# The duration that a list schedule assumes for a float32r product, raised to the step between products in the trace

## The chip, the cores and the metric

The kernel runs on one core of one Trainium2 chip. The metric is the device time of one execution in microseconds (us), the median of several runs. Lower is better. The core's engines are called by the profile's short names: PE (TensorE, matrix products; PEld is its weight load), DVE (VectorE), ACT (ScalarE), POOL (GpSimd) and SP (SyncE, which here only issues DMAs).

## The reference, cut to what matters

Two transformer blocks follow each other on 256 tokens of width 1024, each block two layers deep, all in float32. A layer of the first block is a feed-forward part, a mixer of four kinds of attention, and a second feed-forward part; a layer of the second block is a mixer of three kinds of attention and one feed-forward part.

```python
def first_block(x, ...):
    for l in range(2):
        x = x + 0.5 * swiglu(rms_norm(x, ffn1_norm[l]), gate1[l], up1[l], down1[l])
        h = rms_norm(x, mix_norm[l]) @ w_in[l]          # 12 pieces: q, k, v of four attentions
        o = concatenate([neighborhood, differential, grouped_query, dilated])
        x = x + o @ w_out[l]
        x = x + 0.5 * swiglu(rms_norm(x, ffn2_norm[l]), gate2[l], up2[l], down2[l])
def second_block(x, c, ...):
    for l in range(2):
        ...  # modulated norm, forget-gate / block-sparse / latent attention, swiglu
def swiglu(h, w_gate, w_up, w_down):
    return (silu(h @ w_gate) * (h @ w_up)) @ w_down
```

## The kernel before, in words

**Products.** Every weight tile is loaded as float32 (`raw`), cut into a high part `whi` (ACT, a cast to float32r) and a low part `wlo` (DVE, `raw - whi`), and the activations are held in two parts as well (`xh`, `xl`). One float32 product is then three float32r products into one PSUM bank (`mm3`): `whi,xh`, `whi,xl`, `wlo,xh`, nearly all 128 x 128 x 512. A weight unit is numbered in the order of use; `WStream` loads three units ahead and splits them in halves of 128 x 1024.

**Stages.** In the feed-forward parts PE runs long rows of products. In a mixer of the first block (two in the program, at about 205 to 345 us and 715 to 860 us of the span; "mixer 0" and "mixer 1" below) the in-projection's products are interleaved with the attention. A chunk of the in-projection goes through `prep`: ACT copies it out (`qk`) and squares it (`qksq`), DVE sums (`ss`, `ms`), POOL multiplies by the gain and takes a power (`rs`), DVE multiplies by `rs`, POOL applies the rotary embedding (`rot`, then `qk` again), PE transposes it (`tp<-ident,qk`), and ACT and DVE split the transpose into high and low part (`qkT`). A head then is a job: PE scores (`att<-qkT`, six products of 256 columns, three per token tile), DVE row maxima (`nm`, or `e` with a bias), ACT exponentials (`pd` or `p`), PE transposes of those, an ACT copy (`pt`), PE products with the values (`att<-V,pt`), and DVE scaling into `o`. The differential heads have two score tiles each and a norm of their own (`ov`, `ovs`, `dss`, and one more POOL power `rs`).

**What sets the order.** The program is first only recorded: `Plan.add` (line 114) stores each operation with its dependencies and a duration in ns from `Plan.cost` (line 145). `Plan.order` (line 182) is a list schedule over that record: for each engine it keeps a clock `now`, and an operation can start at the later of that clock, its inputs' ends plus a hop between engines (`HOP`), and the time its buffer comes free; among the operations that could start within `DELTA` = 60 ns of the earliest, the one of highest priority goes. `Plan.priorities` runs the schedule three times and takes each time the priorities from a backward pass (`backward`) over the same durations. `Plan.issue` (line 300) then issues everything in that order; every recorded instruction has line 304. Each engine works through its own list in order and waits on semaphores. So a duration in `cost` never reaches the chip; it decides only which operation stands before which on each engine.

The lines that the change touches (`self.cold` is a constant tile of the warm-up products, `F32R` is float32r; a product that is neither is plain float32):

```python
if eng == "tensor":
    if method == "transpose":
        return 109, 0, None
    n = kw["rhs"].shape[-1]
    ...
    if kw["rhs"].dtype == F32R:
        return n / 2.4 + 2.5, 0, None
    return 2 * max(107, n / 1.2 + 2), 0, None
```

Of the kernel before, what the change touches and what calls it, by code (L numbers as in the profile page):

```python
# [72 lines left out]
class Plan:  # L73
# [26 lines left out]
    def add(self, eng, method, args, kw):  # L100
# [39 lines left out]
        deps.discard(-1)  # L140
        deps.discard(i)
        cost, after, table = self.cost(eng, method, args, kw, aps)
        self.ops.append([eng, method, args, kw, sorted(deps), sorted(touch), cost, after, table])

    HOP = {"tensor": {"vector": 196, "scalar": 197}, "scalar": {"tensor": 258, "vector": 131, "gpsimd": 169},
           "vector": {"tensor": 254, "scalar": 128, "gpsimd": 155, "vector": 127}, "gpsimd": {"vector": 60, "tensor": 136, "scalar": 100, "gpsimd": 102}}

    def cost(self, eng, method, args, kw, aps):

        if method == "dma_start":  # L150
            return (1000 if eng == "gpsimd" else 475), 4 * int(np.prod(list(args[0].shape))) / 360, None
        n = max(int(np.prod(list(a.shape)[1:])) for k, a in aps)
        psum = any(a.space == PSUM for _, a in aps)
# [4 lines that stand above are left out]
            if kw["rhs"] is self.cold:  # L158
                return 4 * max(107, n / 1.2 + 2), 0, None
            if kw["rhs"].dtype == F32R:  # L160
                return n / 2.4 + 2.5, 0, None
            return 2 * max(107, n / 1.2 + 2), 0, None
        if eng == "scalar":
            extra = 93 * sum(1 for k, _ in aps if k in ("bias", "scale", "accum_out"))
            f = args[2] if len(args) > 2 else kw.get("func")
            return 0.833 * n + (52 if psum else 94) + extra, 0, "silu" if f == AF.Silu else "exp" if f in (AF.Exp, AF.Ln) else None
        if eng == "vector":
            fast = method in ("tensor_copy", "tensor_scalar", "memset") and not psum
            scalars = sum(1 for k, _ in aps if k not in (0, 1, "out", "in_")) if method == "tensor_scalar" else 0
            scalars += sum(1 for k, _ in aps if k == 2) if method == "scalar_tensor_tensor" else 0  # L170
            return n * (0.52 if fast else 1.042) + 68 + 62 * scalars, 0, None
        if eng == "gpsimd":
            if kw.get("op") == ALU.pow:
                return 300 + 165 * n, 0, None
            return 148 + (3.15 if method == "tensor_copy" else 2.11) * n, 0, None
        return 60, 0, None
# [1491 lines left out]
```

## Time and profile before

| | |
|---|---|
| median of 3 runs | 1653.28 us (1652.83 to 1656.73) |
| the profiled execution | 1654.43 us, its span 1652.7 us |
| PE busy | 1627.0 us, 98% of the span |
| DVE, ACT, POOL busy | 1085.4, 842.3, 167.9 us |
| mean granted TensorE clock | 0.989 of 2.4 GHz |
| bytes moved by DMA | 335.78 MB, 203 GB/s |

The span runs from the first to the last instruction of the profiled execution; 1.7 us of its time lie outside. A clock of 1.00 in a stretch is 2.4 GHz, 0.50 is 1.2 GHz, and a number between them is the mean of a stretch that has both. The time that an engine stands idle is put down to whatever released it.

### The profile page before, as it was taken

To read this page: it belongs to the slowest core of one execution; us is meant where nothing else is said; L and a number is where in the kernel's file an instruction comes from. 1 tells how busy PE (TensorE), PEld (TensorE's weight loads), DVE (VectorE), ACT (ScalarE), POOL (GpSimd) and SP (SyncE) were. 2 spreads that over 40 slices of the span, in tenths; PEclk is the share of its full clock that TensorE was granted. 3 is DMA by queue.
4 is the path that set the end of the run, shared out by engine and by line. 5 is a ranking of instruction groups with operands and counts; after the bars stand their busy time and mean duration, and the time that the engine had idled before them with its cause. 6 is when DMAs were issued, how large, how long until landed. Compare 5 with 4: busy or idle time off the path is not lost.

```text
span 1652.7 us, 21333 instructions
## 1 busy us (share of the span) xinstructions
PE 1627.0 (98%) x7912; PEld 1347.2 (82%) x7912; DVE 1085.4 (66%) x1956; ACT 842.3 (51%) x1384; POOL 167.9 (10%) x205
## 2 busy tenths in 40 slices
PE   9989999999999999999999999999999999999998
PEld 7868877888888888877788888888888888888886
DVE  6557778577777877777757645656755476585553
ACT  6544456554434444455554444576644358664442
POOL 0000056000000000035400000120000012000000
PEclk9989999999999999998899999999999999999999
DMA  8687762257776777763328645451645445245451
GB/s 305 221 268 283 264 220 103 77 224 301 267 293 245 300 293 267 289 220 120 110 75 311 245 178 195 171 180 53 242 180 202 153 162 207 101 171 202 176 203 51
DMA packets 81884, 335.78 MB, mean 203 GB/s; under 512 B 17136, under 2 KB 19700, under 8 KB 50676
## 3 DMA queue, kind: packets, MB, share of 16 engines
q1 hardware_dynamic: 81780, 334.42, 55.7%
q8 instruction: 62, 1.02, 0.2%
q14 instruction: 42, 0.34, 0.1%
HBM read 333.29 MB, written 2.84 MB: 203 GB/s over the span
## 4 chain that ended last, share of the span: by engine, by line
PE 92%; DVE 3%; POOL 2%; DMA 1%; issue 1%; ACT 1%; SPq 0%; POOLq 0%; DVEq 0%; ACTq 0%
PE mm L304 54%; PE y L304 27%; PE att L304 6%; PE tp L304 6%; DMA raw<-in_gu 1%; DVE wlo L304 1%; POOL rs L304 1%; POOL qk L304 0%; POOL rot L304 0%; DVE o L304 0%; DVE qk L304 0%; DVE ms L304 0%; DVE xl L304 0%; SPq L304 0%; DMA t5t<-in_t_table 0%
## 5 line engine op out<-in xcount | busy, mean ns | idle before, releaser
L304 DVE TENSOR_TENSOR wlo<-raw,whi 128x1024 fp32r<-128x1024 f32 (+2 forms) x516 | 607.2, 1211 | 263.2 <-ACT whi L304 261.4
L304 ACT CAST whi<-raw 128x1024 fp32r<-128x1024 f32 (+2 forms) x516 | 513.4, 1038 | 316.3 <-PE mm L304 132.1
L304 PE MATMUL mm<-whi,xh 128*128 128x512 f32 (+2 forms) x1376 | 547.0, 398 | 2.5 <-ACT whi L304 1.5
L304 PE MATMUL mm<-wlo,xh 128*128 128x512 f32 (+2 forms) x1376 | 537.3, 391 | 0.7 <-DVE wlo L304 0.7
L304 PE MATMUL mm<-whi,xl 128*128 128x512 f32 (+2 forms) x1376 | 534.8, 390 | 1.6 <-DVE xl L304 1.6
L304 PEld LDWEIGHTS mm<-whi,xl 128*128 128x128 f32 x1376 | 259.9, 189 | 55.7 <-DVE xl L304 2.9
L304 PEld LDWEIGHTS mm<-whi,xh 128*128 128x128 f32 x1376 | 259.9, 189 | 55.3 <-ACT whi L304 2.3
L304 PEld LDWEIGHTS mm<-wlo,xh 128*128 128x128 f32 x1376 | 260.4, 189 | 50.5 <-DVE wlo L304 1.6
L304 PE MATMUL y<-whi,hth 128*128 128x512 f32 x528 | 206.9, 393 | 0.0
L304 PE MATMUL y<-wlo,hth 128*128 128x512 f32 x528 | 206.6, 391 | 0.0
L304 PE MATMUL y<-whi,htl 128*128 128x512 f32 x528 | 206.5, 391 | 0.0
L304 POOL TENSOR_TENSOR rs<-rs,mhalf 128x1 f32<-128x1 f32 x28 | 27.2, 972 | 1267.2 <-DVE rs L304 1267.2
L304 ACT ACTIVATE sil<-mm 128x256 f32<-128x256 f32 x110 | 42.2, 384 | 210.4 <-PE mm L304 209.7
L304 DVE CUSTOM_DVE_ANT_0 ada<-ada,act 128x512 f32<-128x512 f32 x192 | 128.5, 688 | 17.3 <-DMA ada<-in_ada 16.9
L304 PEld LDWEIGHTS y<-wlo,hth 128*128 128x128 f32 x528 | 99.7, 189 | 21.6 <-issue 1.3
L304 PEld LDWEIGHTS y<-whi,htl 128*128 128x128 f32 x528 | 99.7, 189 | 20.9
L304 PEld LDWEIGHTS y<-whi,hth 128*128 128x128 f32 x528 | 99.5, 189 | 20.7 <-ACT whi L304 0.2
L304 DVE TENSOR_TENSOR hch<-mm,sil 128x256 f32<-128x256 f32 x110 | 46.3, 421 | 78.9 <-ACT sil L304 78.5
L304 PE MATMUL att<-qkT 64*128 64x256 f32 (+6 forms) x368 | 65.6, 321 | 1.8 <-DVE qkT L304 1.5
L304 POOL TENSOR_TENSOR rs<-ms,mhalf 128x2 f32<-128x2 f32 (+3 forms) x34 | 50.9, 1499 | 135.8 <-DVE ms L304 134.2
L304 PEld LDWEIGHTS att<-V,pt 128*128 128x128 f32 x448 | 59.5, 196 | 6.3 <-ACT pt L304 2.3
L304 PE MATMUL att<-V,pt 128*128 128x65 f32 (+1 forms) x448 | 60.0, 273 | 1.9 <-ACT pt L304 1.9
(158 smaller groups left out, 1388.1 us busy)
## 6 DMA issues: line engine op xcount, KB each, us to landing
raw<-in_gu SPq DMA_DIRECT2D x127, 1024.0 KB, 4.9
raw<-in_dn SPq DMA_DIRECT2D x66, 1024.0 KB, 4.9
ada<-in_ada SPq DMA_DIRECT2D x192, 256.0 KB, 5.3
raw<-in_in SPq DMA_DIRECT2D x32, 1024.0 KB, 4.8
raw<-in_out SPq DMA_DIRECT2D x16, 1024.0 KB, 4.8
row<-moddram SPq DMA_DIRECT2D x12, 512.0 KB, 6.8
raw<-in_in2a SPq DMA_DIRECT2D x4, 840.0 KB, 4.2
raw<-in_gu SPq DMA_DIRECT2D x6, 512.0 KB, 6.1
```

Of the source, the lines that this page charges most:

```text
L304: getattr(getattr(self.nc, eng), method)(*args, **kw)
```

## The change

One constant in the planner's table is raised. For a product of 512 columns the assumed duration goes from 215.8 to 226.6 ns, for 256 columns from 109.2 to 120.0 ns. No instruction, tile or loop is added or removed; the order on the engines is computed anew.

```diff
             if kw["rhs"].dtype == F32R:
-                return n / 2.4 + 2.5, 0, None
+                return n / 2.4 + 13.3, 0, None
             return 2 * max(107, n / 1.2 + 2), 0, None
```

Three places where the order differs follow. Numbers behind names count tiles and units.

On PE in mixer 0, at the end of the third in-projection chunk (`mm_438`, `mm_459` is the next one), the four transposes of the second differential chunk `qk_424` stand so (- before, + now):

```order
 L304 MATMUL mm_438<-whi38_427,xh_74 128x512
 L304 MATMUL mm_438<-wlo38_428,xh_74 128x512
+L304 MATMUL tp_439<-ident_60,qk_424 128x128 x4
 L304 MATMUL mm_438<-whi38_427,xl_75 128x512
-L304 MATMUL mm_459<-whi37_421,xh_74 128x512
-L304 MATMUL mm_459<-wlo37_422,xh_74 128x512
-L304 MATMUL mm_459<-whi37_421,xl_75 128x512
-L304 MATMUL tp_439<-ident_60,qk_424 128x128 x4
 L304 MATMUL mm_459<-whi37_421,xh_74 128x512
```

The transposes have moved four products forward. In mixer 1 the same four stand one product further forward than before.

On PE in mixer 1, the scores of the third and fourth differential head (four groups of six `att<-qkT`), among products of the units 119 (`whi_1285`, `wlo_1286`) and 120 (`whi_1291`, `wlo_1292`). Before:

```order
L304 MATMUL mm<-whi_1291,xh 128x512
L304 MATMUL att<-qkT 128x256 x6
L304 MATMUL mm<-wlo_1292,xh 128x512
L304 MATMUL att<-qkT 128x256 x6
L304 MATMUL mm<-whi_1291,xl 128x512
L304 MATMUL att<-qkT 128x256 x6
L304 MATMUL mm<-whi_1291,xh 128x512
L304 MATMUL att<-qkT 128x256 x3
L304 MATMUL tp<-ident,pd 128x128 x2
L304 MATMUL att<-qkT 128x256 x2
L304 MATMUL tp<-ident,pd 128x128 x2
L304 MATMUL att<-qkT 128x256
```

and now:

```order
L304 MATMUL att<-qkT 128x256 x6
L304 MATMUL mm<-whi_1285,xh 128x512
L304 MATMUL att<-qkT 128x256 x6
L304 MATMUL mm<-wlo_1286,xh 128x512
L304 MATMUL mm<-whi_1285,xl 128x512
L304 MATMUL mm<-whi_1285,xh 128x512
L304 MATMUL mm<-wlo_1286,xh 128x512
L304 MATMUL mm<-whi_1285,xl 128x512
L304 MATMUL att<-qkT 128x256 x2
L304 MATMUL tp<-ident,pd 128x128 x4
L304 MATMUL att<-qkT 128x256 x10
```

Between the first and the last of these 24 scores stood three products, and now stand six; the scores come half a unit earlier.

On POOL in mixer 1, the norms of the last two differential heads (`rs_1374`, `rs_1394`) against the grouped-query chunk `qk_1414` (gain, power `rs_1424`, `rot`, `qk`) stand so:

```order
+L304 TENSOR_TENSOR rs_1374<-ms_1373,mhalf_96 128x2
 L304 TENSOR_TENSOR qk_1383<-rot_1406,rot_1407 128x12x16 x2
+L304 TENSOR_TENSOR rs_1394<-ms_1393,mhalf_96 128x2
 L304 TENSOR_TENSOR qk_1414<-qk_1414,gain1_1_205 128x256
 L304 TENSOR_TENSOR qk_1414<-qk_1414,gain1_1_205 128x128
-L304 TENSOR_TENSOR rs_1374<-ms_1373,mhalf_96 128x2
 L304 TENSOR_TENSOR rs_1424<-ms_1423,mhalf_96 128x6
 L304 TENSOR_TENSOR rot_1431<-qk_1414,rope1_61 128x384
-L304 TENSOR_TENSOR rs_1394<-ms_1393,mhalf_96 128x2
 L304 TENSOR_TENSOR rot_1432<-qk_1414,rope1_61 128x384
```

The power `rs_1394` no longer stands between the two `rot`, but before the whole chain of `qk_1414`.

## Rows read from the trace of the kernel before

**Rows 1.** The page: busy time of each engine; shares of the chain that ended last.
```profile
PE 1627.0 (98%) x7912; PEld 1347.2 (82%) x7912; DVE 1085.4 (66%) x1956; ACT 842.3 (51%) x1384; POOL 167.9 (10%) x205
...
PE 92%; DVE 3%; POOL 2%; DMA 1%; issue 1%; ACT 1%; SPq 0%; POOLq 0%; DVEq 0%; ACTq 0%
```

**Rows 2.** The waits of PE: who was waited for, us in total, times, longest.
```profile
PE tp L304 <- DMA t5t<-in_t_table: 5.8, 1, 5.8
PE tp L304 <- POOL qk L304: 4.0, 2, 2.2
PE att L304 <- ACT pt L304: 1.9, 1, 1.9
...
PE att L304 <- DVE qkT L304: 1.5, 2, 1.0
```

**Rows 3.** Stretches of 50 us: busy by engine (instructions), granted clock, DMA share, GB/s.
```profile
50.00:100.00 50.00, 44.20 (x185) 34.94 (x184) 22.64 (x33) 24.65 (x31) 0.00 (x0) 0.90 0.67 233
...
1100.00:1150.00 50.00, 50.00 (x306) 42.71 (x305) 28.57 (x103) 31.94 (x74) 2.09 (x3) 1.00 0.24 85
```

**Rows 4.** PE's timeline in mixer 1: a score group, and two products at half clock later.
```profile
762.43 0.97 PE L304 MATMUL att<-qkT 32*128 32x256 f32 x6
...
769.13 0.63 PE L304 MATMUL mm<-whi,xh 128*128 128x512 f32 x1
769.56 0.63 PE L304 MATMUL mm<-wlo,xh 128*128 128x512 f32 x1
```

**Rows 5.** Stretches of 5 us in mixer 1, columns as in rows 3.
```profile
765.00:770.00 5.00, 5.00 (x16) 3.17 (x16) 4.19 (x10) 2.53 (x9) 1.26 (x2) 0.56 0.00 0
770.00:775.00 5.00, 5.00 (x32) 4.73 (x31) 2.74 (x13) 3.18 (x12) 1.86 (x1) 0.76 0.00 0
...
785.00:790.00 5.00, 4.03 (x18) 2.67 (x18) 5.00 (x12) 3.19 (x6) 4.89 (x7) 1.00 0.16 64
...
800.00:805.00 5.00, 5.00 (x19) 3.89 (x20) 1.79 (x7) 2.56 (x5) 1.41 (x2) 0.50 0.21 88
805.00:810.00 5.00, 5.00 (x14) 3.83 (x14) 1.46 (x6) 0.91 (x2) 1.64 (x1) 0.50 0.00 0
```

**Rows 6.** PE's timeline in a feed-forward part: start, us; 24 products apart.
```profile
67.19 0.39 PE L304 MATMUL y<-whi,hth 128*128 128x512 f32 x1
...
72.63 0.39 PE L304 MATMUL mm<-whi,xh 128*128 128x512 f32 x1
```

**Rows 7.** PE's timeline in mixer 1, at the longest wait of the last in-projection stretch.
```profile
799.87 1.97 PE L304 MATMUL att<-V,pt 128*128 128x65 f32 x8 [1.85 <-ACT pt L304]
```

**Rows 8.** ACT's timeline there: the copy that PE waits for.
```profile
799.23 0.59 ACT L304 COPY pt<-tp 128x512 f32<-128x512 f32 x1
```

**Rows 9.** DVE's timeline there, in brackets its own wait.
```profile
793.73 3.16 DVE L304 TENSOR_TENSOR wlo<-raw,whi 128x1024 fp32r<-128x1024 f32 x2
797.48 1.22 DVE L304 SCALAR_TENSOR_TENSOR o<-ov,rs,og 128x64 f32<-128x64 f32 x2 [0.59 <-POOL rs L304]
798.62 0.41 DVE L304 TENSOR_TENSOR qkT<-tp,qkT 128x256 fp32r<-128x256 f32 x1
```

**Rows 10.** POOL's timeline in mixer 1: two pairs of rot, then the place of rows 7.
```profile
731.85 0.86 POOL L304 TENSOR_TENSOR rot<-qk,rope 128x128 f32<-128x128 f32 x2 [0.87 <-DVE qk L304]
...
745.99 2.71 POOL L304 TENSOR_TENSOR rot<-qk,rope 128x128 f32<-128x128 f32 x2 [0.86 <-DVE qk L304]
...
793.88 1.93 POOL L304 TENSOR_TENSOR rot<-qk,rope 128x384 f32<-128x384 f32 x1 [0.77 <-DVE ms L304]
795.76 1.68 POOL L304 TENSOR_TENSOR rs<-ms,mhalf 128x2 f32<-128x2 f32 x1
```

**Rows 11.** A stretch of mixer 0, columns as in rows 3.
```profile
247.00:255.00 8.00, 7.70 (x41) 5.46 (x39) 7.79 (x17) 6.56 (x22) 5.07 (x6) 1.00 0.38 131
```

**Rows 12.** PE's timeline at the transposes of the second differential chunk, both mixers.
```profile
239.06 0.66 PE L304 MATMUL tp<-ident,qk 128*128 128x128 f32 x4 [1.86 <-POOL qk L304]
...
750.75 0.66 PE L304 MATMUL tp<-ident,qk 128*128 128x128 f32 x4 [2.16 <-POOL qk L304]
```

## The prediction

> **What bounds the kernel now.** The page comes first: PE is busy for 98% of the span and carries 92% of the chain that ended last [rows 1]. An order of instructions cannot shorten a product, so the change can only touch what PE does not spend on products at full clock. Two views size that. The waits of PE name four that matter, 5.8 + 4.0 + 1.9 + 1.5 = 13.2 us [rows 2]; the span less the busy time is 25.7 us [rows 1], the rest of it being the start, the end and waits under a microsecond. The stretches of 50 us add what no wait shows: stretches in which PE counts as busy while the granted clock is below 1.00, such as 0.90 between 50 and 100 us; a mixer of the second block stands at 50.00 busy and 1.00 [rows 3]. A product takes twice as long at half clock (0.43 us from start to start, 769.13 to 769.56 [rows 4], against 0.23), so a stretch loses its length times what is missing from 1.00: mixer 1 loses 5 x 0.44 + 5 x 0.24 = 3.4 us between 765 and 775 and 2 x 5 x 0.50 = 5.0 us between 800 and 810 [rows 5]. The mixers of the first block are where order matters: waits and half clock both sit there, apart from the one wait on a small DMA.
>
> **The constant itself.** Two products that stand 24 apart start at 67.19 and 72.63 [rows 6]: (72.63 - 67.19)/24 = 0.2267 us from start to start. So the new figure, 226.6 ns for 512 columns, is the trace's; the old one is 10.8 ns lower. On the chip every product keeps its 0.2267 us, so this term is zero. The Trainium skill, page "TensorE: Matmul & The Clock Gate", section "Back-to-back issue gap", speaks against the new figure: it gives columns/2.4 + 2.5 ns for a warm array. By it the 24 steps would take an estimated 5.18 us where the trace has 5.44; the measurement decides, and by either the sum below is the same, since the figure only orders work. What the planner changes is its idea of the others: with PE taken as 5% slower, results of ACT, DVE and POOL seem to arrive after fewer products, so transposes and attention products move forward among the products. That takes slack away wherever the other engines are later than planned, and it reshuffles DVE, ACT and POOL too.
>
> **The change place by place.** All terms are PE time; work that moves elsewhere on PE without a wait costs nothing, because the count of instructions is the same.
>
> *Mixer 1, the copy `pt`: -1.9.* PE waits 1.85 us at 799.87 for an ACT copy [rows 7] that starts at 799.23 [rows 8]. ACT has it queued behind a `qkT` cast, which waits for DVE's `qkT` at 798.62; DVE stood before an `o` that waits for POOL's `rs` [rows 9]; and POOL had that power, 795.76 to 797.44, between two `rot`, the first of which ran from 793.88 to 795.81 [rows 10]. The order now puts this power before the whole chain of that chunk, so DVE's `o` is no longer held; and PE has nine products instead of six between the last transposes before and the awaited `att<-V,pt`, 3 x 0.23 = 0.7 us more cover. I take the wait as gone. If the chain were only 0.7 us covered, 1.2 us of it would stay: bounds -0.7 and -1.9. Next late there would be the transposes of the same chunk; they have some twenty products more behind them.
>
> *Mixer 1, the half clock after it: -5.0.* The clock is 0.50 from that wait until 810 [rows 5]. What PE did before it fell was to stand still for 1.85 us. The clock also fell after the wait of 5.8 us (0.90 [rows 3]), but stayed at 1.00 around a wait of 1.0 us (785 to 790 [rows 5]; the wait is DVE's `qkT` [rows 2]). So with the wait goes the fall. Bounds: 0 and -5.0; I take all of it, since nothing else in that stretch stood still.
>
> *Mixer 1, the half clock from 765 on: -3.4.* No wait stands before this fall. What PE did was four groups of six scores (one of them is shown [rows 4]) with three products in all between them; now six products stand there, and half a unit close before. In mixer 0 the same 24 scores stood among five products, and the clock was 1.00 there [rows 11]. Bounds 0 and -3.4; I take -3.4 as nearer to that neighbour, with less trust than the term above.
>
> *Both mixers, the transposes of the second differential chunk: +1.1.* PE waits there for POOL's `qk`, 1.86 and 2.16 us [rows 12]. POOL's own chain stands as before, and the transposes stand four products earlier in mixer 0 and one in mixer 1: 4 x 0.23 + 0.23 = 1.1 us more waiting. The clock falls after both waits already, so I add nothing for it; a longer fall in mixer 0 would be bounded by another 2 us.
>
> *Both mixers, the dilated heads: +0.5.* Before the first dilated scores stand two products fewer, but DVE has fewer small operations ahead of the `qkT` that they wait for; the wait was 1.0 and 0.5 us [rows 2], and I take half a microsecond off it in mixer 1. Behind them DVE's `e` of the second dilated head now stands behind a half `wlo` split, two of which took 3.16 us, 1.6 each [rows 9]. The transposes that need it did not wait before [rows 2], so the new wait is between 0 and those 1.6 us in each mixer; I take 0.5 each, nearer to none, as they had some slack: 2 x 0.5 - 0.5 = +0.5.
>
> *SP and the small DMA: +0.2.* The product on `t5t` stands one product earlier, and the list on SP before it is the same but for two swapped loads well ahead of it, so the 5.8 us [rows 2] become 6.0 and the half clock behind it stays.
>
> *The rest: 0.* In the feed-forward parts and the mixers of the second block single groups move by one to four products. There PE had no waits worth naming (50.00 busy [rows 3]) and DVE and ACT are idle a third and a half of the time [rows 1]; if that cover went, a moved transpose would cost its shift, 0.2 to 0.9 us, in a few places: bound +2. Score groups among the products number 79 instead of 81, bound -1.
>
> The sum: -1.9 - 5.0 - 3.4 + 1.1 + 0.5 + 0.2 = **-8.5 us**. The profiled execution took 1654.43 us, span 1652.7 and 1.7 outside: 1645.9. It lies 1.15 us above the median of the runs, which spread over 3.9 us, so the median's own figure would be 1644.8; I say 1645.4, between them.
>
> **The rivals.** *One fall of the clock stays.* The stretch from 765 on fell with no wait before it, so the trace cannot say that six products are enough. Then -8.5 + 3.4 = -5.1, or 1649. *The waits only move.* Against the first term: POOL and DVE disturb each other. A pair of `rot` took 0.86 us alone and 2.71 beside DVE's splits [rows 10], so the same chain can come out late somewhere else: the gain of 1.9 + 5.0 is spent at another copy, and with 3.4 left against 1.8 lost the result is about -1.6, 1653. *Slower.* The place is the transposes of the second dilated head, behind DVE's `e` and the split before it. If the split and a POOL operation stretch each other, that wait grows from 0.5 us to about 1.9, and from there the clock falls as it did behind the copy [rows 7]: 1.9 + 5.0 = 6.9 us. The two mixers now stand in nearly the same order, so it would come in both: -8.5 - 1.0 + 13.8 = +4.3, or 1658. For it speaks that the order has become tighter; against it that waits of 1.0 us left the clock alone and my bound for this one is 1.6, and that only without any slack. In the Trainium skill, page "SBUF — State Buffer", section "Who interferes with whom", a DVE instruction with two SBUF inputs and a GpSimd instruction that reads SBUF exclude each other for a whole instruction; by that rule, the trace agrees (0.86 against 2.71), and one half split can so hold POOL back once more there. *No effect at all* is out: the order differs at a thousand places.
>
> **How the numbers follow.** The sum 0.45; one fall stays 0.20; waits only move 0.17; slower 0.18. A measurement of this kernel can tell about 0.3% from no change, 5 us. The sum's case lies beyond that nine times in ten (its bounds scatter by 3 us), the second case less than half the time, the third hardly ever: faster 0.49; same 0.31; slower 0.20. The range takes the sum with 5 us more of gain, 1640.5, and on the other side most of the slower case, 1657.
>
> **What would show it.** Right: in mixer 1 no wait of PE on `pt`, clock 1.00 between its differential and its dilated heads and at their end; PE's waits on POOL's `qk` at about 2.8 and 2.4 us; the half clock left only behind those two and behind `t5t`; mean clock about 0.994 (0.011 x 1652.7 = 18.2 us are lost to it now, 8.4 less then). Wrong: half clock in mixer 0 behind its dilated heads, or a wait over 1.5 us on `p`, `pt` or `qkT` in either mixer.

## The result, and the profile of the changed kernel

The change makes the kernel slower: 1664.3 us, median of 13 runs (1656.9 to 1672.3), against 1653.3 for before in runs of the same chip (13 runs, 1650.4 to 1658.9); the ratio is 1.0061, with a 95% interval of 1.0042 to 1.0079. The prediction said 1645.4, at most 1657.0. The profiled execution took 1661.28 us, its span 1659.5.

The page of the changed kernel, busy time of each engine and the shares of the chain that ended last:

```profile
PE 1627.7 (98%) x7912; PEld 1345.8 (81%) x7912; DVE 1080.7 (65%) x1956; ACT 839.7 (51%) x1382; POOL 166.8 (10%) x205
...
PE 86%; DVE 5%; POOL 3%; DMA 3%; issue 2%; ACT 1%; SPq 0%; POOLq 0%; DVEq 0%; ACTq 0%
```

PE has the same work as in [rows 1], but of the chain it now carries 86% instead of 92%; DVE and POOL have 8% instead of 5%. So there are more places at which PE waits for them. The waits of PE in the changed kernel (who was waited for, us in total, times, longest), against [rows 2]:

```profile
PE tp L304 <- DMA t5t<-in_t_table: 6.8, 1, 6.8
PE tp L304 <- POOL qk L304: 4.8, 2, 2.4
PE att L304 <- DVE qkT L304: 2.6, 2, 1.3
PE tp L304 <- POOL mla L304: 2.0, 2, 1.0
PE att L304 <- ACT qkT L304: 1.4, 2, 1.3
...
PE mm L304 <- ACT mla L304: 1.3, 2, 1.0
```

The wait on `pt` is gone, as foreseen. New are 1.3 us on ACT's `qkT` and waits on `mla`, a piece of a projection in the second block that ACT copies out; DVE's `qkT` has grown from 1.5 to 2.6. Stretches of 50 us, columns as in [rows 3], first of the kernel before, then of the changed one:

```profile
250.00:300.00 50.00, 49.50 (x303) 40.91 (x304) 44.06 (x119) 33.00 (x78) 28.88 (x34) 1.00 0.30 107
...
800.00:850.00 50.00, 50.00 (x309) 42.92 (x309) 26.16 (x77) 26.39 (x51) 7.16 (x6) 0.90 0.20 73
...
1350.00:1400.00 50.00, 49.73 (x283) 43.20 (x283) 34.16 (x81) 37.68 (x91) 15.74 (x32) 1.00 0.61 217
```
```profile
250.00:300.00 50.00, 47.44 (x257) 37.56 (x256) 38.31 (x107) 30.12 (x70) 27.12 (x28) 0.93 0.24 85
...
800.00:850.00 50.00, 50.00 (x338) 43.38 (x338) 29.41 (x86) 27.89 (x56) 11.39 (x11) 1.00 0.25 86
...
1350.00:1400.00 50.00, 47.65 (x264) 40.36 (x265) 36.57 (x80) 37.53 (x90) 16.34 (x32) 1.00 0.57 204
```

Mixer 1 is at 1.00 at its end (800 to 850), where before had 0.90. Mixer 0 has lost clock and busy time (250 to 300: 47.44 us busy at 0.93, before 49.50 at 1.00). In the second block PE stands idle for 2.4 us after 1350, where before was practically full.

### The profile page after: what moved, and what is told of

It is laid out like the page before. It is cut to its first block, busy times and chain, and to the rows that moved or that the text cites. A ratio compares the mean times of both kernels' runs of the same rounds, so it can differ in the third digit from the quotient of the medians.

```text
span 1659.5 us, 21320 instructions
## 1 busy us (share of the span) xinstructions
PE 1627.7 (98%) x7912; PEld 1345.8 (81%) x7912; DVE 1080.7 (65%) x1956; ACT 839.7 (51%) x1382; POOL 166.8 (10%) x205
## 4 chain that ended last, share of the span: by engine, by line
PE 86%; DVE 5%; POOL 3%; DMA 3%; issue 2%; ACT 1%; SPq 0%; POOLq 0%; DVEq 0%; ACTq 0%
PE mm L304 50%; PE y L304 25%; PE att L304 6%; PE tp L304 5%; DVE wlo L304 2%; DMA raw<-in_gu 1%; POOL rs L304 1%; POOL rot L304 1%; POOL qk L304 1%; DMA ada<-in_ada 0%; DVE hn L304 0%; DVE x L304 0%; DMA raw<-in_in 0%; SPq L304 0%; DVE xl L304 0%
## 5 line engine op out<-in xcount | busy, mean ns | idle before, releaser
L304 PEld LDWEIGHTS att<-qkT 64*128 64x128 f32 (+3 forms) x368 | 47.3, 189 | 18.9 <-issue 9.4
```

Of the source, the lines that this page charges most:

```text
L304: getattr(getattr(self.nc, eng), method)(*args, **kw)
```

## Where the time went, stage by stage

Since every product is in both programs, a stage can be timed by its last product: its start in one trace less its start in the profile of before, and from that the same difference for the stage ahead. In us, negative is a gain; "new" marks the stages whose order is the changed one. Three kernels of the first experiment stand in the table as well, since they hold the changed order in one part only.

| profile of | first feed-forward, with `t5t` | mixer 0 | feed-forward | mixer 1 | second block | sum |
|---|---|---|---|---|---|---|
| the change | +0.8 new | +7.5 new | +0.9 new | -9.6 new | +7.2 new | +6.8 |
| the change again | -0.8 new | +7.5 new | +0.9 new | -9.8 new | +6.9 new | +4.7 |
| only_layer0 | +2.0 new | +10.7 new | 0.0 new | -5.2 | +0.5 | +8.1 |
| only_layer1 | -0.1 | +1.6 | +0.4 | -11.3 new | +1.0 | -8.4 |
| only_block2 | -0.1 | +3.1 | 0.0 | -2.2 | +6.9 new | +7.8 |

The gain in mixer 1 came, and two losses of about 7 us ate more than it. The entries without "new" show something else: the old order of a mixer scatters by some us from one profile to the next, and the profile of before stands at the fast end in mixer 0 and at the slow end in mixer 1. Over all profiles of this study the old order of mixer 1 stands at 0 to -6.5 (nine profiles, mean -2.6), the new one at -9.6 to -11.3 (four, mean -10.1): a gain of 7.5. In mixer 0 it is 0 to +3.1 (six, mean +1.4) against +7.5 to +10.7 (three, mean +8.6): a loss of 7.2. In the second block the means are +0.4 and +7.0: a loss of 6.6.

In the old order of mixer 0 the scatter comes from a fall of the clock behind the 24 scores of the third and fourth differential head, which stand among five products there. The profile of before has 1.00 at that place [rows 11], and so has before_block2_swap; in the other four profiles of that order the clock falls, as in only_layer1:

```profile
250.00:255.00 5.00, 5.00 (x21) 3.52 (x20) 4.25 (x10) 3.13 (x11) 1.66 (x2) 0.72 0.48 195
255.00:260.00 5.00, 5.00 (x23) 4.31 (x22) 2.56 (x10) 2.14 (x5) 1.86 (x1) 0.60 0.01 3
```

**Mixer 0.** PE at the first scores of the dilated heads, and what follows (the changed kernel's timeline), then two stretches of 5 us:

```profile
275.36 0.38 PE L304 MATMUL att<-qkT 64*128 64x256 f32 x1 [1.26 <-ACT qkT L304]
277.04 0.85 PE L304 MATMUL att<-qkT 64*128 64x256 f32 x5 [1.30 <-DVE qkT L304]
```
```profile
275.00:280.00 5.00, 3.34 (x11) 2.04 (x11) 5.00 (x17) 4.03 (x8) 3.42 (x5) 0.79 0.41 134
280.00:285.00 5.00, 5.00 (x15) 3.39 (x16) 2.89 (x9) 1.05 (x3) 2.14 (x3) 0.52 0.19 79
```

PE stands still twice, 2.56 us in all, while DVE is busy for the whole 5 us; behind that the clock is at half. DVE's timeline shows what the `qkT` stand behind:

```profile
271.31 2.11 DVE L304 SCALAR_TENSOR_TENSOR o<-ov,rs,og 128x64 f32<-128x64 f32 x2
273.34 1.22 DVE L304 TENSOR_TENSOR wlo<-raw,whi 128x1024 fp32r<-128x1024 f32 x1
274.49 0.41 DVE L304 TENSOR_TENSOR qkT<-tp,qkT 128x256 fp32r<-128x256 f32 x1
...
275.02 1.63 DVE L304 TENSOR_TENSOR wlo<-raw,whi 128x1024 fp32r<-128x1024 f32 x1
276.57 0.41 DVE L304 TENSOR_TENSOR qkT<-tp,qkT 128x256 fp32r<-128x256 f32 x1
```

Before has the same instructions in the same sequence here, but DVE reaches them earlier. Both halves of unit 41's split are done there in one piece, 25 us ahead of these scores (first row, before). With the change one of them comes some ten us later and the other inside the chain that leads to these scores, in front of the halves of unit 42 (257.22 and 263.59 are unit 41, the last two unit 42; rows of the changed kernel):

```profile
247.76 2.61 DVE L304 TENSOR_TENSOR wlo<-raw,whi 128x1024 fp32r<-128x1024 f32 x2
```
```profile
257.22 1.21 DVE L304 TENSOR_TENSOR wlo<-raw,whi 128x1024 fp32r<-128x1024 f32 x1
...
263.59 1.22 DVE L304 TENSOR_TENSOR wlo<-raw,whi 128x1024 fp32r<-128x1024 f32 x1
265.06 1.22 DVE L304 TENSOR_TENSOR wlo<-raw,whi 128x1024 fp32r<-128x1024 f32 x1
266.52 1.22 DVE L304 TENSOR_TENSOR wlo<-raw,whi 128x1024 fp32r<-128x1024 f32 x1
```

The order says why: before, all but one of unit 37's products stand ahead of the scores of the first two differential heads; with the change four of them stand among or behind these scores. Unit 41 takes unit 37's buffer, and so its split can only come later.

**The second block.** ACT in its first mixer, before and then with the change, followed in each by POOL's next rotary embedding:

```profile
1076.29 0.48 ACT L304 COPY mla<-mm 128x384 f32<-128x384 f32 x1 [0.17 <-PE mm L304]
1076.66 1.05 ACT L304 CAST whi<-raw 128x1024 fp32r<-128x1024 f32 x1
...
1076.85 0.91 POOL L304 TENSOR_TENSOR rot<-mla,rope 128x128 f32<-128x128 f32 x2 [3.51 <-ACT mla L304]
```
```profile
1075.82 1.07 ACT L304 CAST whi<-raw 128x1024 fp32r<-128x1024 f32 x1
1076.77 0.77 ACT L304 COPY mla<-mm 128x384 f32<-128x384 f32 x2
...
1077.34 1.78 POOL L304 TENSOR_TENSOR rot<-mla,rope 128x128 f32<-128x128 f32 x2 [4.19 <-ACT mla L304]
...
1080.84 0.64 PE L304 MATMUL tp<-ident,mla 128*96 128x128 f32 x4 [1.05 <-POOL mla L304]
```

Before, ACT waited 0.17 us for the product and copied it out at once. With the change half a split stands ahead of the copy, and the copy waits behind 1.07 us of it. (The likely reason, which no run shows: in the plan with longer products that product comes later, so that ACT seems to have time for the split.) POOL starts 0.5 us later, its two `rot` take 1.78 instead of 0.91, and PE waits 1.05. The second mixer has the same exchange. The rest of the 7 us in this block is not one place: the waits of PE there sum to 4.0 us in the two mixers (0.2 before), and the other 3 us stand in no wait that the profile names.

## Experiments

Ratios are against before on the same chip, with the 95% interval. Medians of different rows can be from different chips, where before alone differs by some us (1649.9 to 1654.0), so rows are compared by their ratios.

| kernel | median, us | ratio to before |
|---|---|---|
| the change again | 1661.9 | 1.0065 (1.0042 to 1.0087) |
| only_layer0 | 1661.4 | 1.0048 (1.0032 to 1.0065) |
| only_layer1 | 1646.4 | 0.9958 (0.9939 to 0.9977) |
| only_block2 | 1663.2 | 1.0061 (1.0043 to 1.0080) |
| figure_minus_8 | 1652.2 | 1.0000 (0.9988 to 1.0012) |
| figure_plus_8 | 1656.2 | 1.0016 (1.0004 to 1.0029) |
| figure_plus_24 | 1686.9 | 1.0212 (1.0190 to 1.0234) |
| block2_swap | 1658.9 | 1.0030 (1.0012 to 1.0048) |
| before_block2_swap | 1655.9 | 1.0025 (1.0011 to 1.0039) |
| layer0_chunk_first | 1659.6 | 1.0054 (1.0037 to 1.0070) |
| layer0_split_early | 1656.2 | 1.0030 (1.0018 to 1.0043) |
| layer0_split_behind | 1658.3 | 1.0035 (1.0022 to 1.0047) |
| layer0_all_three | 1655.4 | 1.0012 (0.9998 to 1.0025) |
| before_o_behind | 1653.0 | 1.0006 (0.9991 to 1.0021) |
| mix | 1641.6 | 0.9943 (0.9921 to 0.9964) |
| mix_plus | 1640.7 | 0.9927 (0.9911 to 0.9944) |

### The change in one part of the program

The figure is kept for each recorded product, by the phase that records it (0 to 2 are the first block's first layer, 3 to 5 its second, from 6 on the second block); outside its part a kernel has the order of before, instruction for instruction on PE and POOL, inside it that of the change.

```diff
-                return n / 2.4 + 2.5, 0, None
+                return n / 2.4 + self.gap, 0, None
 ...
             b, l, kind = phases[i]
+            nc.gap = 13.3 if i < 3 else 2.5      # only_layer1: i in (3, 4, 5); only_block2: i > 5
```

> The changed kernel once more, for a second profile of it. Theory (the order has fixed weak places): the profile shows the same places as the first one of it: PE waits 1.3 us on ACT's qkT and 1.3 us on DVE's qkT at the first dilated scores of mixer 0 and the clock is down to about 0.5 for some 6 us behind them; mixer 1 has no wait on pt and a clock of 1.00 from 800 us on; PE waits about 1.0 us on POOL's mla in both mixers of the second block. Time 1657 to 1668. Rival (the falls of the clock change from run to run): same time, but the half clock lies in other places of the span.

> The higher figure only for products of the first block's first layer (feed-forward, mixer 0, feed-forward); the order from about 550 us on is that of before. Theory (the parts add up as the two traces differ): +9.2 us against before, 1662: the 0.8 at t5t, 7.5 in mixer 0, 1.0 in the feed-forward part behind it. My forecast's terms for this part were +1.6, 1655. Rival (falls of the clock come at random, whatever the order): between -4 and +12 with no half clock at the dilated scores of mixer 0.

> The higher figure only for products of the first block's second layer; the order before 550 us and behind the first block is that of before. Theory (the parts add up, and the forecast of mixer 1 was right): -9.5 us against before, 1644, no wait on pt in mixer 1 and clock 1.00 at the end of it. Rival (falls of the clock come at random): between -5 and +5, a half clock elsewhere in mixer 1.

> The higher figure only for products of the second block; the first block's order is that of before. Theory (the parts add up as the two traces differ): +6.6 us against before, 1660, with PE's waits of about 1 us on POOL's mla and on ACT's mla in the two mixers. My forecast had 0 here, bound +2: 1653 to 1655. Rival: the waits come from what the first block leaves behind it, then this part alone costs nothing, 1653.

The second profile of the change shows the first one's waits to a tenth (1.3 and 1.3 us at the dilated scores, 1.1 on `mla`, none on `pt`), so these places are fixed by the order; the half clock behind them moves by some us. The three parts measure +0.48%, -0.42% and +0.61%, in sum +0.67%; the whole measures +0.61 and +0.65%. So the parts add up, and the gain that was forecast is real and stands alone in only_layer1.

The runs say more than their ratios, since the span and the mean granted clock of every execution are on record. The span times (1 - clock) is, as an estimate, the time that half clock cost; what is left is work at full clock and standing still. The means over all executions, against before on the same chip, in us, with 95% intervals:

| kernel | half clock | the rest |
|---|---|---|
| the change again | +0.5 (±3.8) | +10.7 (±1.3) |
| only_layer0 | +4.6 (±3.1) | +3.5 (±2.0) |
| only_layer1 | -7.7 (±3.4) | +0.8 (±1.1) |
| only_block2 | +2.6 (±2.0) | +8.0 (±1.1) |
| block2_swap | -1.3 (±3.0) | +6.4 (±1.0) |
| before_block2_swap | +2.6 (±2.1) | +2.0 (±1.1) |
| layer0_all_three | +2.3 (±2.5) | +0.3 (±1.0) |
| figure_minus_8 | -4.0 (±2.2) | +3.5 (±0.8) |

The gain of only_layer1 is half clock and nothing else. The first layer gives the greater part of it back (+4.6), and the loss of the whole change is the rest: 10.7 us, most of it in the second block, whose mixers stand at 1.00 in every profile of the change. The profile of only_block2, too, has half clock only in the first block, where its order is that of before, and at the end of the span.

### Other figures

The same line with other constants, everywhere in the program:

```diff
-                return n / 2.4 + 2.5, 0, None
+                return n / 2.4 - 8.3, 0, None        # figure_plus_8: + 7.9; figure_plus_24: + 24.1
```

> The assumed duration lowered instead of raised: columns/2.4 - 8.3 ns, 205 ns for 512 columns. Theory (the low figure is slack: the planner puts more products between the close of a chunk and the attention that needs it; here 22.9 us of PE work between the last product of the dilated chunk and its first scores in mixer 0, before 20.9, after the change 19.2): no wait of PE on qkT at the dilated scores of either mixer, and not slower than before, 1645 to 1655. Rival (before is one good order among many, and any other figure draws a worse one): 1658 to 1668, with new waits elsewhere.

> The assumed duration half way: columns/2.4 + 7.9 ns, 221 ns for 512 columns; 20.2 us of PE work between the last product of the dilated chunk and its first scores in mixer 0. Theory (slack): between before and the change, 1655 to 1662, with the wait on qkT at the dilated scores of mixer 0 between 0.5 and 2.6 us. Rival (each figure draws its own order): anywhere from 1645 to 1670.

> The assumed duration raised beyond the trace: columns/2.4 + 24.1 ns, 237 ns for 512 columns; 17.7 us of PE work between the last product of the dilated chunk and its first scores in both mixers. Theory (slack): slower than the change, 1668 to 1680, with waits on qkT at the dilated scores of more than 3 us in mixer 0. Rival (each figure draws its own order): anywhere from 1645 to 1670, no longer waits than with the change.

Over five figures (-8.3, 2.5, 7.9, 13.3, 24.1) the ratio goes 1.0000, 1, 1.0016, 1.0061 to 1.0065, 1.0212. It never falls below 1, as it should not if the low figure of before works as slack, and above the trace's own step the loss grows fast: with 24.1, which costs more than was expected, PE waits 8.7 us for DVE's `xl` alone:

```profile
PE mm L304 <- DVE xl L304: 8.7, 7, 3.0
```

The single places are less orderly than the sum. With -8.3 mixer 0 stands at -3.1 and has no wait at the dilated scores, but mixer 1 has 1.7 and 1.4 us there, although this figure was to give the most cover; and the second block costs +7.4 at -8.3 (3.4 of it one wait on `hn`, a normed activation of DVE) and +6.0 at 7.9. There the order of before is a good one among worse, on both sides of its figure. So the ratio of 1.0000 is two things that cancel, 4.0 us less half clock and 3.5 us more of the rest. With 7.9 no score waits for a `qkT` at all; its waits are 1.5 and 1.3 us on ACT's `p`. With 24.1 the one in mixer 0 is 1.8 us, where more than 3 was expected. The wait at these scores does not scale with the figure.

### The second block: a split in front of a copy

In block2_swap the copy `mla` goes back ahead of the half split in both mixers (ACT alone, two pairs); before_block2_swap does the opposite to before.

```diff
+CAST whi169_1910<-raw169_1830 128x1024
 COPY mla_1864<-mm_1863 128x384
-CAST whi169_1910<-raw169_1830 128x1024
 COPY mla_1866<-mm_1865 128x4x64
```

(as before_block2_swap has it; likewise `whi216` and `mla_2391` in the second mixer)

> The order of only_block2 with two pairs on ACT changed places, one in each mixer of the second block: the copy mla that POOL's rotary embedding waits for stands again ahead of the first half split whi of a unit that is needed much later (1.07 us). Nothing moves on PE, DVE or POOL. Theory (the split in front of the copy makes the wait): PE's wait on POOL's mla falls from 2 x 1.1 us to under 2 x 0.4 and the one on ACT's mla from 0.9 to under 0.3; the two mixers cost 2.5 to 5 us less than in only_block2, 1658 to 1661. Rival (the waits come from PE's own order, which is unchanged here): same waits, 1663.

> The order of before with the two pairs on ACT in the mixers of the second block changed places the other way: the half split whi stands ahead of the copy mla, as the change puts it; nothing else moves. Theory (this pair alone makes the waits on POOL's mla): PE waits about 1.1 us on POOL's mla in both mixers, 2 to 4 us above before, 1655 to 1657. Rival (it takes the new order of PE as well): no wait over 0.4 us, 1653.

PE's waits in the two mixers, first only_block2, then block2_swap, then before_block2_swap:

```profile
PE tp L305 <- POOL mla L305: 2.2, 2, 1.1
PE mm L305 <- ACT mla L305: 0.9, 2, 0.5
```
```profile
PE tp L309 <- ACT mla L309: 1.3, 2, 0.7
PE mm L309 <- DVE wlo L309: 1.3, 1, 1.3
```
```profile
PE tp L308 <- POOL mla L308: 1.2, 1, 1.2
PE mm L308 <- ACT mla L308: 0.7, 2, 0.4
```

The pair makes the wait as was thought: put in, it brings the one on POOL's `mla` in the first mixer and costs 0.25%; taken out, that wait is gone. In the second mixer of before_block2_swap no such wait came, so there the new order of PE is needed as well. In block2_swap the profile gains nothing (+7.1 instead of +6.9, from the same table as above), since the split that stands behind is now late for its own product (1.3 us on `wlo`) and other transposes wait for ACT's `mla`; the runs do gain, from 1.0061 to 1.0030. But most of that gain is half clock (+2.6 against -1.3), and the second block has none of it in either profile; the rest goes only from +8.0 to +6.4. Put in, the pair costs 2.0 us of the rest, and the profile has +1.7 in this block. So the pair is worth about 2 of the 8 us, a quarter. With the new order of PE the waits sum to as much without the pair (3.9 us) as with it (4.0): something else is late then. Which moves on PE make the other three quarters stays open.

### Mixer 0: cover, or a queue

> The order of only_layer0 with one thing moved in mixer 0: the last six products of the chunk that holds the dilated queries stand again ahead of the scores of the third and fourth differential head, and ACT copies that chunk out ahead of those heads' exponentials; the rest as in only_layer0. Theory (12 scores in front of the close of the chunk took 1.8 us of PE time from the cover of the chain that the first dilated scores wait for): their waits fall from 1.2 + 1.3 to under 1.0 us together, the half clock behind them goes, mixer 0 costs 4 to 7 us less than in only_layer0, 1655 to 1658. Rival (the chain is held on DVE and POOL, whose order is unchanged): the waits stay at 2.5 us, 1661.

```diff
+MATMUL mm_459<- unit 38, 6 products
 MATMUL att_471<-qkT x6
-MATMUL mm_459<- unit 38, 1 product
 MATMUL att_472<-qkT x6
-MATMUL mm_459<- unit 38, 5 products
```

My first explanation was PE's: twelve scores had moved ahead of the last six products of the dilated chunk, so its chain had 1.8 us less cover. This did not hold. PE's waits there, in mixer 0:

```profile
PE att L309 <- ACT qkT L309: 1.5, 1, 1.5
PE att L309 <- DVE qkT L309: 1.3, 1, 1.3
```

They are as long as in only_layer0, and the ratio is 1.0054 against 1.0048. The chain is not short of time on PE; it is held on its way. The next three kernels take the splits off that way, by moving unit 41's split back to where before has it, by moving unit 43's behind the two `qkT`, and by all named moves together.

```diff
# layer0_split_early, DVE (ACT: whi41 ahead of the exponentials pd_444; PE: 4 products of unit 37 ahead of att_442)
 TENSOR_SCALAR nm4_447<-nm4_447 128x4
+TENSOR_TENSOR wlo41_476<-raw41_429,whi41_475 128x1024
+TENSOR_TENSOR wlo41_476<-raw41_429,whi41_475 128x1024
 RECIPROCAL rc4_446<-rs4_441 128x4
# layer0_split_behind, DVE
-TENSOR_TENSOR wlo43_546<-raw43_462,whi43_545 128x1024
 TENSOR_TENSOR qkT_454<-tp_537,qkT_453 128x2x128
 TENSOR_TENSOR ov_532<-att_531,rc4_507 128x128
-TENSOR_TENSOR wlo43_546<-raw43_462,whi43_545 128x1024
 TENSOR_TENSOR qkT_456<-tp_537,qkT_455 128x2x128
+TENSOR_TENSOR wlo43_546<-raw43_462,whi43_545 128x1024
+TENSOR_TENSOR wlo43_546<-raw43_462,whi43_545 128x1024
```

> The order of only_layer0 with one weight unit's split put back where before has it: the last four products of unit 37 stand ahead of the differential scores of mixer 0, so that the buffer is free, and both halves of unit 41's split (whi on ACT, wlo on DVE, 1.05 and 1.2 us each) stand ahead of those heads' exponentials and reciprocals, where both engines wait, instead of in front of the dilated chain. Theory (DVE is the queue at the dilated scores, and the deferred splits are 2.4 us of it): PE's waits on qkT there fall from 1.2 + 1.3 to under 1.0 us together; mixer 0 costs 3 to 6 us less than in only_layer0, 1655 to 1658. Rival (the lateness comes from elsewhere): waits above 2 us together, 1660 or more.

> The order of only_layer0 with DVE's two halves wlo of unit 43 behind the two qkT that the first dilated scores of mixer 0 wait for, instead of one in front of each (1.2 and 1.6 us there); nothing else moves. Theory (the same: DVE's queue): PE's waits on qkT fall from 1.2 + 1.3 to under 0.6 us together; 2 to 5 us less than in only_layer0, 1656 to 1659. Rival (the waits only move on, to the first product with unit 43 or to DVE's e): a new wait of 1 us or more behind it, 1661.

> The order of only_layer0 with the moves of layer0_chunk_first, layer0_split_early and layer0_split_behind together. Theory: no wait on qkT over 0.5 us at the dilated scores, and mixer 0 within 3 us of before, 1652 to 1656. Rival (many small places carry the loss): 1658 or more although these waits are gone.

PE's waits in mixer 0 in the three, in this order, with the stretch from 250 to 260 us behind the first and the third:

```profile
PE att L309 <- ACT pd L309: 1.5, 1, 1.5
PE att L309 <- DVE qkT L309: 0.6, 1, 0.6
...
250.00:260.00 10.00, 10.00 (x34) 7.20 (x33) 6.81 (x19) 5.36 (x20) 0.80 (x2) 0.50 0.30 107
```
```profile
PE tp L309 <- ACT p L309: 1.4, 1, 1.4
```
```profile
PE tp L309 <- DVE pd L309: 1.3, 2, 1.0
...
250.00:260.00 10.00, 8.67 (x41) 6.78 (x41) 8.24 (x21) 6.18 (x23) 2.99 (x3) 0.66 0.29 107
```

Either way of taking the splits off shortens the waits on `qkT`, from 2.5 us to 0.6 or to nothing. Each leaves a smaller new wait (1.5 on `pd`, 1.4 on `p`), which is the rival's half of the truth, and the clock can fall elsewhere (0.50 from 250 to 260 us in the first). Their ratios, 1.0030 and 1.0035, are lower than the 1.0048 of only_layer0, but the intervals overlap, so that either move gains by itself is not shown. With all moves the ratio is 1.0012, its interval reaches 1 and lies clear of only_layer0's, and the rest falls from +3.5 to +0.3 us: about three quarters of the layer's loss is in these places. So the dilated scores of mixer 0 wait for DVE's queue. That the splits fill it is shown by both moves; that unit 41's, which the change deferred, lengthened it, by layer0_split_early. Unit 43's stand there in before as well.

### Mixer 1: does the wait bring the low clock?

```diff
-SCALAR_TENSOR_TENSOR o_1272<-ov_1390,rs_1394,og1_1252 128x64
-SCALAR_TENSOR_TENSOR o_1272<-ov_1390,rs_1394,og1_1252 128x64
 TENSOR_TENSOR qkT_1380<-tp_1417,qkT_1379 128x2x128
 RECIPROCAL rc_1419<-att_1418 128x2
 TENSOR_TENSOR qkT_1382<-tp_1417,qkT_1381 128x128
+SCALAR_TENSOR_TENSOR o_1272<-ov_1390,rs_1394,og1_1252 128x64
+SCALAR_TENSOR_TENSOR o_1272<-ov_1390,rs_1394,og1_1252 128x64
```

> The order of before with one move on DVE in mixer 1: the two o that wait for POOL's power rs stand behind the two qkT of the transposes that follow, instead of ahead of them (rows 9). It takes away the cause that the prediction named for the wait of 1.85 us on pt, and nothing else. Theory (the o held the chain back, and the fall of the clock behind the wait comes in some executions only: it was 0.50 for 10 us in the profile of before, 3.5 us long in that of only_block2 and absent in that of only_layer0, each with the same wait of 1.85 us): wait on pt under 0.5 us, median 2 to 5 us below before, 1649 to 1652. The prediction's own step (a fall of 5.0 us always follows): 6.9 us below, 1647. Rival (something else is as late): wait stays above 1 us, no gain.

The wait on `pt` is gone, so its cause was named rightly; but nothing is gained. In its profile the clock falls all the same, a little earlier, behind the 0.97 us on `qkT` that before has as well:

```profile
787.28 0.86 PE L308 MATMUL att<-qkT 64*128 64x256 f32 x5 [0.97 <-DVE qkT L308]
...
790.00:795.00 5.00, 5.00 (x15) 3.31 (x15) 5.00 (x22) 1.81 (x4) 3.49 (x3) 0.50 0.60 210
```

And with the wait in place, in the old order of mixer 1, the fall need not come: only_layer0 first, then only_block2, each with the wait and the stretch behind it.

```profile
811.97 1.11 PE L305 MATMUL att<-V,pt 128*128 128x65 f32 x8 [1.85 <-ACT pt L305]
...
815.00:820.00 5.00, 5.00 (x31) 4.32 (x30) 2.93 (x11) 3.05 (x6) 1.72 (x2) 1.00 0.00 0
```
```profile
802.27 1.57 PE L305 MATMUL att<-V,pt 128*128 128x65 f32 x8 [1.85 <-ACT pt L305]
...
805.00:810.00 5.00, 5.00 (x16) 3.78 (x15) 1.59 (x7) 1.49 (x3) 1.99 (x2) 0.54 0.00 0
```

The same wait of 1.85 us left the clock at 1.00 once, brought it down for part of ten microseconds once (some 7 us, which cost the 3.5 us that the expectation above calls its length), and for all of ten in [rows 5] and in before_block2_swap. In five more profiles with the old order of mixer 1 (block2_swap and the four layer0 kernels) PE waits 0.3 us or less on `pt`, and in each of them the clock was below 1.00 already between 780 and 800 us (0.79 to 0.93), behind the `qkT`. My reading is that a PE at half clock reaches the copy later and finds it done, so that the wait and the fall stand in for each other. What keeps the clock up at the end of mixer 1 in the new order (1.00 in the four profiles of it) is more than this wait; what exactly, stays open.

### A figure for each part

```diff
-            nc.gap = 13.3 if i < 3 else 2.5
+            nc.gap = -8.3 if i < 3 else 13.3 if i < 6 else 2.5
```

and for mix_plus one move on DVE in mixer 1:

```diff
+TENSOR_TENSOR qkT_1314<-tp_1395,qkT_1313 128x2x128
 TENSOR_TENSOR wlo124_1404<-raw124_1320,whi124_1403 128x1024
-TENSOR_TENSOR qkT_1314<-tp_1395,qkT_1313 128x2x128
```

> A figure for each part: columns/2.4 - 8.3 ns in the first block's first layer (as in figure_minus_8), + 13.3 in its second layer (as in the change), + 2.5 in the second block (as in before). Theory (parts add up): against the profile of before -2 to -5 in the first layer, -9.5 in the second, 0 in the second block, so 4 us below only_layer1, 1641 to 1645. Rival (the first layer's gain in the profile of figure_minus_8 was the scatter of one execution): as only_layer1, 1646.

> The kernel mix with one instruction moved: DVE's first half wlo of unit 124 stands behind the second qkT of the dilated chunk of mixer 1 instead of in front of it (1.22 us); PE waits 1.35 us there in mix and the clock is low for 3 us behind it. Theory (a wait that is gone is gained): wait under 0.3 us, 1 to 3 us below mix, 1639 to 1641. Rival (as in before_o_behind the clock falls elsewhere and nothing is gained): as mix, 1641.6.

Both beat before and the change: 1641.6 us (0.9943) and 1640.7 us (0.9927). The stages of mix add up as told: -5.2 up to the end of mixer 0, -9.8 in mixer 1, +0.1 in the second block. Between the two, mixer 1 gains another 1.2 us in the profile and the wait of 1.4 falls to 0.2; the runs' intervals overlap, so that this last step is a gain is not shown by them. In the profile of mix_plus PE is busy for 99% of its span.

## Why the prediction was wrong, step by step

- **What bounds the kernel:** the four waits that were named are not the longest in sum: `xl` (1.6 us) and `whi` (1.5), each with one of 1.1, and `ident` (1.4) were passed over, so the remainder was not all "under a microsecond". No term of the sum uses them.
- **The constant itself, 0:** right. It changes no product; the figure of the trace is still 226.7 ns a step. That the truer figure gives the worse order is the point of the ladder of five figures.
- **The copy `pt`, -1.9:** the wait went, in every profile of the new order, and before_o_behind shows that DVE's `o` behind POOL's power was its cause. As a gain by itself it was mis-sized: taken away alone it is worth nothing that the runs show (1.0006).
- **The half clock after it, -5.0:** the clock is at 1.00 there with the change, but the step's reason fell. "With the wait goes the fall" is not so: the fall came without the wait and the wait without the fall. The place was right, by luck: what keeps the clock up there is another cause, and it stays open.
- **The half clock from 765 on, -3.4:** it came. That fall is in all ten profiles of the old order of mixer 1 (0.50 and 0.87 in before_o_behind) and in none of the four of the new one. The reason did not hold: the neighbour, mixer 0 with five products among the scores, was at 1.00 in the profile of before, but its clock fell in four of six profiles of the same order. Whether six products are what keeps it up was not tested.
- **Mixer 1 in sum:** forecast about -10, measured -9.6 and -9.8 against the profile of before, but -6.9 us (0.42%) in the runs of only_layer1. The terms were sized against one execution, and that one stood at the slow end there; against the mean of nine profiles the gain is 7.5. By the runs all of it is half clock (-7.7, forecast -8.4).
- **Transposes of the second differential chunk, +1.1:** right in kind; 2.4 and 2.4 us instead of the 2.8 and 2.4 that were named, so +0.8.
- **Dilated heads, +0.5: this is the first step that failed.** I saw that DVE had "fewer small operations" in front of the `qkT` and booked a gain, and set a bound for `e`. In mixer 0 the waits on those very `qkT` became 2.6 us, with half clock behind, and the stage lost 7 us. I had compared the rows next to the scores, which are the same on DVE, and not asked where unit 41's split had gone; it had moved from a place 25 us ahead into the chain. The layer0 kernels show it for about three quarters of the layer's loss.
- **SP and the small DMA, +0.2:** 6.6 to 7.7 us with the changed order (seven profiles) against 5.8 to 6.6 with the old one (six): about +0.8, so the term was too small.
- **The rest, 0, bound +2: this is the second step that failed.** It reasoned from the shares, PE full and ACT idle half of the time. The second block lost 6.6 us by the profiles and 8.0 by the runs. About 2 of them are one pair on ACT: a split of 1.07 us put in front of a copy that was due in 0.17 us, and idle time elsewhere does not help the copy behind it. The other three quarters go with the new order of PE, and their places stay open.
- **The rivals:** "slower" had the right kind of mechanism, a split in front of a step that PE needs, but less than half of the size (+4.3 against some 10 us); its place (`p`, behind `e`, in both mixers) was wrong, and 0.18 was too little for it. The range ended just below that rival's number and had no room for losses in two parts at once.
- **The signs named for "wrong":** one came, half clock in mixer 0 behind its dilated heads; the other did not, since none of the waits there reached 1.5 us. The mean clock is 0.991 in the profile and 0.989 over all 13 executions, as before, not 0.994.

By the means of the profiles the change is worth +7.2 in mixer 0, -7.5 in mixer 1, +6.6 in the second block and about +1 elsewhere: some 7 us, where the runs have 10 (0.61%). The missing 3 us are half clock: it cost the profiled execution of the change 14.9 us, and its 13 executions 18.0 in the mean.

## What to carry to other kernels

A duration in a planner's table is a source of slack as much as a fact: the figure that the trace gives made the worse order here, and a figure for each part of the program made the best one, so try the knob per stage. When an order is re-computed, follow on each in-order engine the long instructions that nobody is waiting for (splits, prefetches), and see where they went relative to the short ones that the bounding engine waits for. And price a fall of the clock from several profiles, or from the granted clock of all executions: one execution can hold it at its worst, and a neighbour that was spared once proves little.

## What the runs showed of the hardware

That half clock follows a wait only sometimes was not expected: with the same order and the same 1.85 us of standing still, 10 us of half clock, part of it, and none. It is the same behind the 24 scores in mixer 0, with waits of 0.4 us at most in front of them: the clock fell in four profiles of six. The old order of mixer 1 scattered by 6.5 us over nine profiles. In the Trainium skill, page "TensorE: Matmul & The Clock Gate", section "What's actually happening", the count of slow products at a kernel's start is said to differ from run to run; these runs show the like in the middle of one. The other is the pair of POOL and DVE: two `rot` took 0.91 us in one order, beside small operations on DVE, and 1.78 in the next, half a microsecond later, beside a split on DVE. [rows 10] had this already; what is new is that a shift of 0.5 us can so double a step of the chain.
